# Attention probabilities of a two-layer hybrid block: the division by their sum, on the scalar engine instead of the vector engine

## The chip, the core and the metric

The kernel runs on one core of a Trainium2 chip. The metric is the device time of one execution in microseconds (us), of which the median of three runs is taken; it is 1531.88 us (1525.68 to 1533.71). One further execution was taken with the hardware profiler; all stretches and durations below are from that one. The engines of the core have short names: PE is the matrix engine (PEld its weight loads, which overlap with its multiplications), DVE the vector engine, ACT the scalar engine, POOL the GpSimd engine, SP the engine that issues most DMAs. Each engine works through its own instructions in the order in which they were written, and waits on semaphores for the others.

## The reference

Two layers over 256 latent tokens and 256 context tokens with 1024 channels, batch 1, float32. Each layer has three mixer branches (a bidirectional mLSTM, grouped-query attention and neighbourhood attention), their merge, and a convolutional feed-forward part. The change lies in the softmax that both attention branches use:

```python
def attend(q, k, v):
    s = jnp.einsum('bqkgd,bskd->bkgqs', q, k).astype(jnp.float32) * (HEAD_DIM ** -0.5)
    p = jax.nn.softmax(s, axis=-1).astype(v.dtype)
    return jnp.einsum('bkgqs,bskd->bqkgd', p, v)
...
def na_latent(q, k, v, kc, vc, rpb):
        ...
        s_win = jnp.einsum('bqhd,brqjhd->bhqrj', q_row, k_win).astype(jnp.float32) * scale + bias.astype(jnp.float32)
        s_ctx = jnp.einsum('bqhd,bshd->bhqs', q_row, kc).astype(jnp.float32) * scale
        s = jnp.concatenate([s_win.reshape(B, H, GRID_W, wr * wc), s_ctx], axis=-1)
        p = jax.nn.softmax(s, axis=-1).astype(v.dtype)
```

In both layers the latent tokens attend to latent and context tokens (512 keys); in layer 0 alone the context tokens also attend to themselves (256 keys).

## The kernel before, in words

**Large matrix products.** Every weight is loaded in float32 as a tile `raw` (two 128-row blocks of 512 columns, or one of 1024) and split into two float32r parts: `whi`, a cast by ACT (L200, `split_hi`), and `wlo`, the rest `raw - whi` by DVE (L204, `split_lo`). Each product is then three matmuls (L315, `mm3`): high by high, and the two mixed ones. One weight tile with its matmuls is a **piece**; `run` (L165) goes through all pieces in program order, and keeps the splits up to two pieces ahead of the matmuls that use them. After the matmuls of a piece, `run` advances a queue of side work by one step (`step`, L265). So side work stands between the pieces, on every engine, in the order in which Python wrote it: nothing is reordered later.

**Attention as side work.** `g_attend` (L651) is such a side task. Its **units** are a pair of heads by a block of 128 queries (512 keys), or in layer 0 also a pair of heads by all 256 context queries (`qt is None`, handled as two halves of 128x256 per head). Neighbourhood attention (`g_na`) and grouped-query attention (`g_gqa`) have 8 units of the first kind in each layer, and 4 of the second kind in layer 0. One step of the task t does three things, in this order:

- `pv` for unit t-2: the products of transposed probabilities `pT` with the values (L722), then the high part of the result on ACT (`yhi` or `y`, L725), and the low part on DVE (L726).
- `norm_transp` for unit t-1: four transposes on PE for each head of the pair (L708), from the probabilities `pr` into a PSUM bank, which is copied out as `pT` by ACT for the first head (L711) and by DVE for the second (L713).
- `scores` for unit t: the score products (L672, or L669 for the context units) into one bank for each head; then for each head on DVE the bias (L677, neighbourhood attention of the latent units only) and the negative maximum `mn` (L681), and on ACT the exponential with its row sum (L684); and after both heads, for each head, the reciprocal `rc` of the sum on DVE (L689) and the product `pr * rc` (L691).

Five banks are written in a step and four exist for side work (`bank(False)`). The second score product of a step therefore takes a bank that was used earlier in the same step: mostly the one of the first head's transposes, which is free once ACT has copied `pT` (L711), in some units the one of `pv`, which is free after L726.

**A piece and its step, in the order of the queues.** After a step of the attention, `run` splits the weights of a later piece: next on ACT stands `whi` (L200), next on DVE `wlo` (L204). In layer 0, pieces that only compute modulation vectors (L448, three DVE products of a 128x1024 weight tile with a vector) are spread among the others; they stand on DVE between the softmax of a step and the next `wlo`. When a block of pieces ends, ACT (or DVE) empties its banks; for the block of keys, values and gates of `g_gqa` these are four copies `akv` (L1156) on ACT, between `whi` and the next `yhi`.

**Draining.** A block that needs the output of a side task calls `finish`, which runs the rest of its steps with no pieces between them. In layer 0 the last context units of `g_gqa` are run so (the projection of that branch needs them).

In layer 0 a piece has matmuls for 512 token columns, in layer 1 the parts that only latent tokens need have 256, so pieces there are about half as long on PE, while a step of the attention is as long as in layer 0.

Of the kernel before, what the change touches and what calls it, by code (L numbers as in the profile page):

```python
# [13 lines left out]
ALU = mybir.AluOpType  # L14
# [34 lines left out]
class Builder:  # L49
# [601 lines left out]
    def g_attend(self, units, qk, v_of, y):  # L651


        nc = self.nc

        def scores(u):
            p, qt, c0, bias = u
            out = []
            bt = None
            if bias is not None:  # L660
                bt = self.t((128, 2, 256), name="nab")
                nc.gpsimd.dma_start(out=bt, in_=bias)
            bs = []
            for par in range(2):
                b = self.bank(False)
                q, k = qk(p, par)
                if qt is None:
                    for i in range(2):
                        nc.tensor.matmul(b[:, 256 * i:256 * i + 256], q[:, c0 + 128 * i:c0 + 128 * i + 128],  # L669
                                         k[:, 0:256], start=True, stop=True)  # L670
                else:
                    nc.tensor.matmul(b, q[:, c0:c0 + 128], k[:, 0:512], start=True, stop=True)  # L672
                bs.append(b)
            for par in range(2):
                b = bs[par]
                if bt is not None:
                    nc.vector.tensor_tensor(b[:, 256:512], b[:, 256:512], bt[:, par, :], op=ALU.subtract)  # L677
                mn = self.sm([128, 4], name="mn")
                ns = 2 if qt is None else 1
                w = 512 // ns  # L680
                nc.vector.tensor_reduce(mn[:, 0:ns], b.rearrange("p (n w) -> p n w", n=ns), axis=AX.X, op=ALU.min)  # L681
                pt = self.t(name="pr")
                for i in range(ns):
                    nc.scalar.activation(out=pt[:, w * i:w * i + w], in_=b[:, w * i:w * i + w], func=ACTF.Exp, scale=-1.0,  # L684
                                         bias=mn[:, i:i + 1], accum_out=mn[:, 2 + i:3 + i])
                rc = self.sm([128, 2], name="rc")
                out.append((pt, mn, rc, ns, w))
            for pt, mn, rc, ns, w in out:
                nc.vector.reciprocal(rc[:, 0:ns], mn[:, 2:2 + ns])  # L689
                for i in range(ns):  # L690
                    nc.vector.tensor_scalar(pt[:, w * i:w * i + w], pt[:, w * i:w * i + w], rc[:, i:i + 1], None,  # L691
                                            op0=ALU.mult)
            return [o[0] for o in out]

        def norm_transp(u, i):
            pts = res.pop(i)
            pT[i] = [transp(u, pts[par], par) for par in range(2)]

        def transp(u, pt, par):
            qt = u[1]  # L700
            b = self.bank(False)
            for i in range(4):
                if qt is None:

                    o = (i % 2) * 256 + (i // 2) * 128
                else:
                    o = i * 128
                nc.tensor.transpose(b[:, o:o + 128], pt[:, 128 * i:128 * i + 128], self.I)  # L708
            pT = self.t(name="pT")
            if par == 0:  # L710
                nc.scalar.copy(pT, b)  # L711
            else:
                nc.vector.tensor_copy(pT, b)  # L713
            return pT

        def pv(u, pTs):
            p, qt, c0, _ = u
            nkt, w = (2, 256) if qt is None else (4, 128)
            b = self.bank(False)
            for kt in range(nkt):  # L720
                for par in range(2):
                    nc.tensor.matmul(b[64 * par:64 * par + 64, 0:w], v_of(p, par, kt), pTs[par][:, w * kt:w * kt + w],  # L722
                                     start=kt == 0, stop=kt == nkt - 1)
            hi, lo = y[0][:, p, c0:c0 + w], y[1][:, p, c0:c0 + w]
            nc.scalar.copy(hi, b[:, 0:w])  # L725
            nc.vector.tensor_tensor(lo, b[:, 0:w], hi.bitcast(F32), op=ALU.subtract)  # L726

        n = len(units)
        res, pT = {}, {}
        for t in range(n + 2):  # L730
            if t >= 2:
                pv(units[t - 2], pT.pop(t - 2))
            if 1 <= t <= n:
                norm_transp(units[t - 1], t - 1)
            if t < n:
                res[t] = scores(units[t])
            yield
# [847 lines left out]
```

## Time and profile before

| | us |
|---|---|
| median of three runs | 1531.88 (1525.68 to 1533.71) |
| profiled execution, its own time | 1527.63 |
| span of its instructions | 1525.9 |
| DVE busy | 1090.3 (71%) |
| ACT busy | 732.1 (48%) |
| stretches with steps of neighbourhood attention | about 99 to 205 (layer 0), 1038 to 1093 (layer 1) |
| stretches with steps of grouped-query attention | about 265 to 363 (layer 0), 1122 to 1178 (layer 1) |

How the views are read: a *group* is all instructions of one source line, engine and shape, with its busy time, the mean duration of one in ns, and the idle time of the engine in front of it with what ended it. The *chain* is followed back from the last instruction of the span to what released each step. The *timeline* has start and duration of single instructions; neighbouring equal ones are merged (x4), and an idle time stands in brackets. Line numbers are those of the kernel before.

### The profile page before, as it was taken

How to read it: one execution, taken by the hardware profiler on the slowest of the kernel's cores; microseconds unless marked ns; L12 is line 12 of the kernel's file. 1: busy time of each engine (PE TensorE's matmuls, PEld its weight loads, DVE VectorE, ACT ScalarE, POOL GpSimd, SP SyncE). 2: the span in 40 equal slices, each digit the busy share in tenths (PEclk: the TensorE clock that was granted, in tenths of full speed). 3: DMA queues.
4: the chain of work that ended last, by engine and by line, in shares of the span. 5: the costliest groups of instructions: out<-in, count | busy, mean ns of one | idle time of the engine just before them, and what ended most of it. 6: DMA issues, size and time to landing. Idle time of an engine off the chain costs nothing.

```text
span 1525.9 us, 22991 instructions
## 1 busy us (share of the span) xinstructions
PE 1450.4 (95%) x8689; PEld 1251.4 (82%) x8689; DVE 1090.3 (71%) x1974; ACT 732.1 (48%) x1343; POOL 215.8 (14%) x312
## 2 busy tenths in 40 slices
PE   6999998998999899999999999999999998899997
PEld 3877787776888778888888887887887898899986
DVE  3548787777755887888767888736886347778874
ACT  4334441443435247644334555634554355666663
POOL 2000012003412031111011000000020230212110
PEclk9999999998999899999999999999999999999999
DMA  9624344331543356545554687733442344455662
GB/s 336 218 84 144 111 133 131 96 111 56 153 152 117 111 176 213 164 140 164 165 166 164 211 275 256 254 119 97 114 148 79 91 122 137 161 182 182 216 201 90
DMA packets 103807, 238.08 MB, mean 156 GB/s; under 512 B 8416, under 2 KB 18720, under 8 KB 103568
## 3 DMA queue, kind: packets, MB, share of 16 engines
q1 hardware_dynamic: 99472, 224.56, 45.7%
q0 software_dynamic: 4224, 12.05, 3.0%
q8 instruction: 68, 1.11, 0.3%
q14 instruction: 43, 0.35, 0.1%
HBM read 235.50 MB, written 1.08 MB: 155 GB/s over the span
## 4 chain that ended last, share of the span: by engine, by line
PE 71%; DVE 16%; ACT 5%; issue 4%; DMA 3%; POOL 1%; DVEq 0%; SPq 0%; ACTq 0%; POOLq 0%
PE bank L315 59%; DVE wlo L204 4%; PE bank L708 2%; PE bank L672 2%; PE bank L722 2%; DMA raw<-in_w_down 2%; DVE ta L1337 1%; DVE jnk L448 1%; ACT whi L200 1%; DVE D L1020 1%; ACT D L1003 1%; DVE raw L448 1%; PE bank L417 1%; PE bank L669 1%; DMA raw<-in_w_mod 1%
## 5 line engine op out<-in xcount | busy, mean ns | idle before, releaser
L204 DVE TENSOR_TENSOR wlo<-raw,whi 128x1024 fp32r<-128x1024 f32 (+1 forms) x330 | 410.9, 1260 | 154.0 <-ACT whi L200 152.9
L315 PE MATMUL bank<-HThi,whi 128*128 128x256 f32 (+1 forms) x1408 | 466.0, 331 | 7.8 <-DVE sig L1182 2.9
L315 PE MATMUL bank<-HThi,wlo 128*128 128x256 f32 (+1 forms) x1408 | 461.2, 328 | 7.7 <-DVE wlo L204 7.7
L315 PE MATMUL bank<-HTlo,whi 128*128 128x256 f32 (+1 forms) x1408 | 460.9, 327 | 0.5 <-DVE HTlo L591 0.5
L200 ACT CAST whi<-raw 128x1024 fp32r<-128x1024 f32 (+1 forms) x330 | 335.8, 1037 | 200.8 <-PE bank L315 60.7
L315 PEld LDWEIGHTS bank<-HThi,whi 128*128 128x128 f32 x1408 | 270.8, 192 | 39.2 <-issue 13.4
L315 PEld LDWEIGHTS bank<-HThi,wlo 128*128 128x128 f32 x1408 | 270.9, 192 | 27.6 <-DVE wlo L204 9.2
L315 PEld LDWEIGHTS bank<-HTlo,whi 128*128 128x128 f32 x1408 | 270.9, 192 | 18.9 <-DVE HTlo L591 1.2
L315 PE MATMUL bank<-whi,xs 128*128 128x512 f32 x528 | 160.1, 381 | 2.5 <-DVE o L623 1.6
L1337 DVE SCALAR_TENSOR_TENSOR ta<-bank,cw,ta 128x255 f32<-128x255 f32 (+2 forms) x224 | 110.7, 527 | 52.6 <-ACT ta L1334 48.6
L315 PE MATMUL bank<-whi,HThi 128*128 128x512 f32 (+1 forms) x384 | 143.3, 373 | 0.3 <-DVE sig L1182 0.2
L315 PE MATMUL bank<-wlo,HThi 128*128 128x512 f32 (+1 forms) x384 | 139.6, 364 | 0.8 <-DVE wlo L204 0.8
L315 PE MATMUL bank<-whi,HTlo 128*128 128x512 f32 (+1 forms) x384 | 139.4, 363 | 0.0
L315 PEld LDWEIGHTS bank<-whi,xs 128*128 128x128 f32 x528 | 99.8, 189 | 18.4 <-DVE o L623 2.0
L315 PE MATMUL bank<-wlo,xs 128*128 128x512 f32 x264 | 100.8, 382 | 4.3 <-DVE wlo L204 4.2
L448 DVE SCALAR_TENSOR_TENSOR raw<-raw,CB 128x1024 f32<-128x1024 f32 x80 | 102.2, 1277 | 1.7
L1357 POOL TENSOR_TENSOR hT<-ta 128x256 f32<-128x256 f32 (+1 forms) x48 | 60.2, 1257 | 303.5 <-ACT ta L1356 303.1
L684 ACT ACTIVATE pr<-bank,mn 128x512 f32<-128x512 f32 (+1 forms) x96 | 58.4, 614 | 91.4 <-DVE mn L681 85.0
L1334 ACT ACTIVATE ta<-bank,cw 128x256 f32<-128x256 f32 (+1 forms) x96 | 61.2, 646 | 84.3 <-PE bank L315 82.5
L315 PEld LDWEIGHTS bank<-whi,HThi 128*128 128x128 f32 x384 | 72.8, 190 | 21.6 <-issue 11.4
L315 PEld LDWEIGHTS bank<-wlo,HThi 128*128 128x128 f32 x384 | 72.9, 190 | 9.5 <-DVE wlo L204 1.5
L315 PEld LDWEIGHTS bank<-whi,HTlo 128*128 128x128 f32 x384 | 72.8, 189 | 8.7
(233 smaller groups left out, 1807.6 us busy)
## 6 DMA issues: line engine op xcount, KB each, us to landing
raw<-in_w_in SPq DMA_DIRECT2D x112, 512.0 KB, 3.7
raw<-in_w_up SPq DMA_DIRECT2D x96, 512.0 KB, 4.6
raw<-in_w_modT SPq DMA_DIRECT2D x80, 512.0 KB, 4.5
raw<-in_w_down SPq DMA_DIRECT2D x66, 512.0 KB, 4.6
raw<-in_w_branch SPq DMA_DIRECT2D x24, 512.0 KB, 3.7
raw<-in_w_out SPq DMA_DIRECT2D x24, 512.0 KB, 4.3
raw<-in_w_mod SPq DMA_DIRECT2D x16, 512.0 KB, 10.5
nab<-in_nabias POOLq DMA_DIRECT2D x16, 256.0 KB, 3.2
```

What stands on the lines that cost most here:

```text
L200: nc.scalar.copy(p.hi, p.raw.tile[:, p.k0:p.k0 + p.kn, :])
L204: nc.vector.tensor_tensor(p.lo, p.raw.tile[:, p.k0:p.k0 + p.kn, :], p.hi.bitcast(F32), op=ALU.subtract)
L315: nc.tensor.matmul(out, l, self.woven(r), start=first and i == 0, stop=last and i == 2)
L417: nc.tensor.matmul(st["b"][32 * g:32 * g + 32, 256 * ch:256 * ch + 256], w, rt[:, g, :], start=c == 0, stop=c == 1)
L448: nc.vector.scalar_tensor_tensor(o, rt[:, 0, a:b], 1.0, self.CB[:, s, a:b], op0=ALU.mult, op1=ALU.mult, accum_out=acc)
L672: nc.tensor.matmul(b, q[:, c0:c0 + 128], k[:, 0:512], start=True, stop=True)
L684: nc.scalar.activation(out=pt[:, w * i:w * i + w], in_=b[:, w * i:w * i + w], func=ACTF.Exp, scale=-1.0, bias=mn[:, i:i + 1], accum_out=mn ...
L708: nc.tensor.transpose(b[:, o:o + 128], pt[:, 128 * i:128 * i + 128], self.I)
L722: nc.tensor.matmul(b[64 * par:64 * par + 64, 0:w], v_of(p, par, kt), pTs[par][:, w * kt:w * kt + w], start=kt == 0, stop=kt == nkt - 1)
L1334: nc.scalar.activation(out=tv, in_=bv, func=ACTF.Identity, scale=cw[:, ch, 1:2], bias=cw[:, ch, 3:4])
L1337: nc.vector.scalar_tensor_tensor(o, x, cw[:, ch, t:t + 1], o, op0=ALU.mult, op1=ALU.add)
L1357: nc.gpsimd.tensor_tensor(hv, av, ta, op=ALU.mult)
```

## The change

The product L691 moves from DVE to ACT. Its inputs, its output and its place in the program text stay, so on ACT it stands behind the exponentials of both heads of the unit, and ahead of everything that is written later. The product has a scale that is a column of numbers in memory (one for each partition), not a constant.

```diff
             for pt, mn, rc, ns, w in out:
                 nc.vector.reciprocal(rc[:, 0:ns], mn[:, 2:2 + ns])
                 for i in range(ns):
-                    nc.vector.tensor_scalar(pt[:, w * i:w * i + w], pt[:, w * i:w * i + w], rc[:, i:i + 1], None,
-                                            op0=ALU.mult)
+                    nc.scalar.mul(pt[:, w * i:w * i + w], pt[:, w * i:w * i + w], rc[:, i:i + 1])
             return [o[0] for o in out]
```

Later lines of the changed kernel have numbers that are lower by one.

ACT, neighbourhood attention in layer 1, around the copies `akv`, before:

```order
L684 ACTIVATE pr,mn<-bank,mn 128x512 x2
L200 CAST whi<-raw 128x1024
L1156 COPY akv<-bank 128x272 x4
L725 CAST y<-bank 128x128
L711 COPY pT<-bank 128x512
L684 ACTIVATE pr,mn<-bank,mn 128x512 x2
L200 CAST whi<-raw 128x1024
```

The same place on ACT, after:

```order
L684 ACTIVATE pr,mn<-bank,mn 128x512 x2
L691 ACTIVATE pr<-pr,rc 128x512 x2
L200 CAST whi<-raw 128x1024
L1155 COPY akv<-bank 128x272 x4
L724 CAST y<-bank 128x128
L710 COPY pT<-bank 128x512
L684 ACTIVATE pr,mn<-bank,mn 128x512 x2
L691 ACTIVATE pr<-pr,rc 128x512 x2
L200 CAST whi<-raw 128x1024
```

Two products stand between the exponentials of a unit and the next cast `whi`; the casts, the copies `akv`, and the `y` and `pT` of the next step stand behind them. No load of a function table is added on ACT.

DVE, one turn of the neighbourhood attention in layer 1, before:

```order
L677 TENSOR_TENSOR bank<-bank,nab 128x256
L681 TENSOR_REDUCE mn<-bank 128x1
L677 TENSOR_TENSOR bank<-bank,nab 128x256
L681 TENSOR_REDUCE mn<-bank 128x1
L689 RECIPROCAL rc<-mn 128x1
L691 TENSOR_SCALAR pr<-pr,rc 128x512
L689 RECIPROCAL rc<-mn 128x1
L691 TENSOR_SCALAR pr<-pr,rc 128x512
L204 TENSOR_TENSOR wlo<-raw,whi 128x1024
L726 TENSOR_TENSOR y<-bank,y 128x128
L713 COPY pT<-bank 128x512
```

The same turn on DVE, after:

```order
L677 TENSOR_TENSOR bank<-bank,nab 128x256
L681 TENSOR_REDUCE mn<-bank 128x1
L677 TENSOR_TENSOR bank<-bank,nab 128x256
L681 TENSOR_REDUCE mn<-bank 128x1
L689 RECIPROCAL rc<-mn 128x1 x2
L204 TENSOR_TENSOR wlo<-raw,whi 128x1024
L725 TENSOR_TENSOR y<-bank,y 128x128
L712 COPY pT<-bank 128x512
```

The products are gone from between the reciprocals, and `wlo`, which needs `whi`, still stands ahead of the low part `y`, the copy `pT` and the bias of the next unit. The orders of PE, POOL and SP do not change.

## The prediction

> **What bounds the kernel now.** I read the page first: the busy times, then the chain that ended last.
>
> ```profile
> PE 1450.4 (95%) x8689; PEld 1251.4 (82%) x8689; DVE 1090.3 (71%) x1974; ACT 732.1 (48%) x1343; POOL 215.8 (14%) x312
> PE 71%; DVE 16%; ACT 5%; issue 4%; DMA 3%; POOL 1%; DVEq 0%; SPq 0%; ACTq 0%; POOLq 0%
> ```
>
> PE holds the end nearly everywhere; DVE holds 16% of the chain, ACT 5%. So the question is not what DVE and ACT do in sum, but in which stretch of the attention one of them keeps PE waiting. Second, the groups of the product and of the ACT operations nearest to its new form:
>
> ```profile
> L691 DVE TENSOR_SCALAR pr<-pr,rc 128x512 f32<-128x512 f32 x64 | 31.2, 487 | 2.2
> L691 DVE TENSOR_SCALAR pr<-pr,rc 128x256 f32<-128x256 f32 x32 | 9.9, 351 | 0.6
> L1356 ACT ACTIVATE ta<-ta 128x512 f32<-128x512 f32 x18 | 11.4, 631 | 13.7 <-DVE ta L1337 13.7
> L1356 ACT ACTIVATE ta<-ta 128x256 f32<-128x256 f32 x30 | 12.3, 417 | 15.8 <-DVE ta L1337 15.4
> L1037 ACT ACTIVATE H<-bank,mr 128x128 f32<-128x128 f32 x24 | 8.7, 363 | 48.9 <-DVE mr L1035 47.5 <-PE bank L1031 0.7
> L725 ACT CAST y<-bank 128x128 fp32r<-128x128 f32 x16 | 4.3, 270 | 16.8 <-PE bank L722 16.7
> L1334 ACT ACTIVATE ta<-bank,cw 128x512 f32<-128x512 f32 x36 | 28.1, 781 | 47.1 <-PE bank L315 47.1
> L1174 ACT ACTIVATE sig<-bank 128x512 f32<-128x512 f32 x24 | 13.6, 603 | 10.2 <-PE bank L315 10.2
> ```
>
> DVE spends 31.2 + 9.9 = 41.1 us on the product. Third, the waits of PE: the product ends 9.1 us of PE's idle time.
>
> ```profile
> PE bank L708 <- DVE pr L691: 9.1, 11, 1.6
> ```
>
> Fourth, the chain and the timelines of the attention stages, quoted where they are used.
>
> **The change: the price of one product on ACT.** The trace has no product of this form on ACT. An in-place function on 128x512 took 0.631 us with constant scale (L1356). A column as scale costs 0.363 - 0.270 = 0.09 (L1037 against L725, same size, both from PSUM). I take 0.631 + 0.09 = 0.72, and 0.417 + 0.09 = 0.51 for 128x256; the lower bound is 0.63, the upper is 0.78 (L1334, two columns). ACT starts the next operation about 0.1 before the end of the last: three L1174 took 1.59,
>
> ```profile
> 194.75 1.59 ACT L1174 ACTIVATE sig<-bank 128x512 f32<-128x512 f32 x3
> ```
>
> that is (1.59 - 0.60)/2 = 0.50 each beside a duration of 0.60. A product thus holds ACT for 0.62 (0.53 to 0.68), a small one for 0.41, and `whi` moves back by 2 x 0.62 = 1.24 us in a unit of 512 keys. ACT has room for it in sum: 64 x 0.62 + 32 x 0.41 = 53 us on an engine that is 48% busy. What counts is the order.
>
> **Layer 1, neighbourhood attention: the main term.** Chain, one turn on PE, and the same turn on DVE and ACT:
>
> ```profile
> 1070.32 1.42 PE bank L672 x4
> ...
> 1076.57 1.42 PE bank L672 x4
> ```
>
> ```profile
> 1071.41 0.43 DVE L677 TENSOR_TENSOR bank<-bank,nab 128x256 f32<-128x256 f32 x1 [0.36 <-PE bank L672]
> ...
> 1075.56 1.23 DVE L204 TENSOR_TENSOR wlo<-raw,whi 128x1024 fp32r<-128x1024 f32 x1 [0.25 <-ACT whi L200]
> 1076.70 0.29 DVE L726 TENSOR_TENSOR y<-bank,y 128x128 fp32r<-128x128 f32 x1
> 1076.90 0.68 DVE L713 COPY pT<-bank 128x512 f32<-128x512 f32 x1
> 1077.66 0.43 DVE L677 TENSOR_TENSOR bank<-bank,nab 128x256 f32<-128x256 f32 x1
> ```
>
> ```profile
> 1073.81 0.69 ACT L684 ACTIVATE pr<-bank,mn 128x512 f32<-128x512 f32 x1 [0.34 <-DVE rc L689]
> 1074.39 0.19 ACT L684 ACTIVATION_READ_ACCUMULATOR pr<-bank,mn 128x1 f32 x1
> 1074.48 1.04 ACT L200 CAST whi<-raw 128x1024 fp32r<-128x1024 f32 x1
> ```
>
> PE's turn is 1076.57 - 1070.32 = 6.25. Beside it runs a ring through DVE and ACT: bias to second exponential 2.40, exponential to `whi` 0.67, `whi` to `wlo` 1.08, then `wlo` 1.14, `y` 0.20 and `pT` 0.60 (DVE, too, starts the next some 0.08 early), and the next bias may start: 6.09. Its slack against PE is only 0.16. The removed DVE products are not in this ring (DVE then waits 0.25 for `whi` anyway), so nothing is gained; the two ACT products are: 6.09 + 1.24 = 7.33, or **1.08 more than PE's turn**. From the third unit's bias to the eighth's there are five such turns:
>
> ```profile
> 1052.17 0.43 DVE L677 TENSOR_TENSOR bank<-bank,nab 128x256 f32<-128x256 f32 x1 [0.36 <-PE bank L672]
> ...
> 1083.91 0.43 DVE L677 TENSOR_TENSOR bank<-bank,nab 128x256 f32<-128x256 f32 x1 [0.18 <-PE bank L672]
> ```
>
> They now take 31.74, and will take 5 x 7.33 = 36.65: +4.9. The two units ahead, whose casts are half as wide, add about 0.85 by the same walk (the first waits for both exponentials ahead of its product, then a ring of 6.3 against 6.1). Of the 5.75 on DVE, PE absorbs about 0.25 at the last unit: **+5.5 us**, 4.1 to 6.3 with the bounds of the product. Behind it PE runs on without gaps until the next chain, so nothing gives it back.
>
> **Layer 1, grouped-query attention.** No bias, so the ring is shorter. Chain of a turn:
>
> ```profile
> 1133.52 1.06 PE bank L672 x4
> ...
> 1139.51 1.42 PE bank L672 x4
> ```
>
> ```profile
> 1129.43 0.69 ACT L684 ACTIVATE pr<-bank,mn 128x512 f32<-128x512 f32 x1 [0.91 <-DVE mn L681]
> 1130.11 0.68 ACT L684 ACTIVATE pr<-bank,mn 128x512 f32<-128x512 f32 x1
> 1130.77 1.04 ACT L200 CAST whi<-raw 128x1024 fp32r<-128x1024 f32 x1
> ```
>
> ```profile
> 1128.71 1.28 DVE L681 TENSOR_REDUCE mn<-bank 128x1 f32<-128x512 f32 x2
> ```
>
> PE's turn is 5.99. The ring, from `mn` to `mn`: 0.72 to the first exponential, 0.68 to the second, 0.66 to `whi`, and the same rest, 1.08 + 1.14 + 0.20 + 0.60: 5.08; with 1.24 it is 6.32. In the first turn the second score product waits for `pT` of ACT, which I estimate at 0.3 to spare and which comes 1.24 later (about +1.0); the three turns behind add 0.33 each, less the slack of their score products (+0.5): **+1.5** (0.7 to 2.2). The last turns are those of whole-width pieces, as in layer 0 below, and lose nothing.
>
> **Layer 0, neighbourhood attention.** At its start DVE is the bound, and here the product does go: the second one stood between `rc` and the modulation product.
>
> ```profile
> 112.57 0.16 DVE L689 RECIPROCAL rc<-mn 128x1 f32<-128x1 f32 x1 [0.31 <-ACT pr L684]
> 112.77 0.49 DVE L691 TENSOR_SCALAR pr<-pr,rc 128x512 f32<-128x512 f32 x1
> 113.17 0.69 DVE L448 SCALAR_TENSOR_TENSOR jnk<-raw,CB 128x512 f32<-128x512 f32 x1
> ```
>
> That is 0.4 for each of two units: -0.8 on DVE. The third has no modulation product, so its `wlo` waits for `whi`: +1.24 - 0.8 = +0.4. Then the unit with the copies `akv`, where ACT has no gap:
>
> ```profile
> 127.14 1.25 ACT L1156 COPY akv<-bank 128x272 f32<-128x272 f32 x4
> ...
> 128.40 0.64 ACT L711 COPY pT<-bank 128x512 f32<-128x512 f32 x1
> ```
>
> ```profile
> 129.09 0.29 PEld L672 LDWEIGHTS bank<-nk,nq 64*128 64x128 f32 x2 [0.78 <-ACT pT L711]
> ```
>
> The second score product already waits 0.78 for `pT`; `pT` moves by 0.4 + 1.24: **+1.65** (1.1 to 2.0). After that PE's turn is 8.84,
>
> ```profile
> 154.24 1.02 PE bank L708 x8
> ...
> 163.08 1.02 PE bank L708 x8
> ```
>
> and the ring, 7.33, stays below it: 0. At the end of the grouped-query attention three units run with nothing between them.
>
> ```profile
> 345.02 0.17 DVE L689 RECIPROCAL rc<-mn 128x2 f32<-128x2 f32 x1
> 345.23 0.62 DVE L691 TENSOR_SCALAR pr<-pr,rc 128x256 f32<-128x256 f32 x2
> ```
>
> DVE ends the four products 0.8 after the last exponential frees `rc`; on ACT they take 4 x 0.41 + 0.1 = 1.7. Against +0.9 in each of the last two stands the 0.5 that DVE gains in the first, and what overlaps with the transposes: **+0.8** (0 to 1.5).
>
> **Sum.** 5.5 + 1.5 + 1.65 + 0.8 = +9.5 us, bounds 5.9 and 12.0. The profiled execution's own time is 1527.63, so it would be 1537.1. The median of the runs shown is 4.25 above it; on that, 1531.9 + 9.5 = **1541.4**, which I forecast.
>
> **The rivals.**
>
> - *Not slower: the rings don't bind.* If the products cost ACT less, or the split ran further ahead, so that the added 1.24 fitted, only the gain at the start (-0.8) and a stall at the copies would be left: -1.2 to +1, about 1531.9. For it: ACT is idle half the time. It decides at 0.16 us: as long as two products lengthen the ring by less, PE keeps its 6.25. Against it: the lower bound is 2 x 0.53.
> - *Faster: DVE's relief reaches the end.* If every wait of PE for the product (9.1) went and its DVE stretches shrank by two units' products (2), it would be 1520.8. Against it: PE's wait is for the probabilities, which still have to be multiplied, and later than before.
> - *Every product shows at the end with its extra length*: 64 x (0.72 - 0.49) + 32 x (0.51 - 0.35) = 20 us, 1551.9. Against it: most units stand where PE's turn is over 8 us. The Trainium skill (ScalarE: Activation LUTs, section Rules for kernel authors) gives multiplications to VectorE as the faster engine; taken as a rule for this kernel it means this case, while the rows agree on the two prices but show most of them hidden.
>
> That the products do move, with no added table load, stands in the order of the built program.
>
> **How the numbers follow.** Forecast 0.68, rings don't bind 0.18, all shown 0.07, relief 0.07. A measurement tells 0.5% (7.7 us) from no change. Of the forecast's range 5.9 to 12.0 about four fifths lies above 7.7, so slower by over 0.5% is 0.68 x 0.8 + 0.07 = 0.61, within 0.5% 0.18 + 0.14 = 0.32, faster 0.07. The range takes in the forecast with its bounds, the spread of the runs before, and the unbound rings: 1530 to 1548; the relief and the case in which all shows are left out.
>
> **What would show it.** Right: in layer 1 the biases L677 stand 7.2 to 7.5 apart instead of 6.25, DVE's idle time ahead of `wlo` grows from 0.25 to over 1 with ACT `whi` as its end, PE waits for ACT `pr` ahead of the transposes, and the stretch from 1038 to 1093 is 4 to 6 us longer; the product takes 0.70 to 0.73. Wrong: biases 6.25 apart, or a product under 0.6; or a gain in layer 0 that outweighs layer 1, with DVE's chain from 104 to 121 shorter by more than 1 and no new wait at 129. The forecast falls if `wlo` does not wait for `whi` in that ring.

## The result, and the profile after

| | before | after |
|---|---|---|
| median of nine runs each, us | 1526.60 (1524.46 to 1533.71) | 1538.64 (1535.00 to 1545.81) |
| ratio, 95% interval | | 1.0076 (1.0058 to 1.0094) |
| span of the profiled execution, us | 1525.9 | 1535.9 |

The change costs 0.76%, by the ratio 11.6 us (8.9 to 14.4); the two profiled spans are 10.0 apart. First the engines' sums on the page of the changed kernel:

```profile
PE 1461.1 (95%) x8689; PEld 1253.5 (82%) x8689; DVE 1047.4 (68%) x1878; ACT 779.9 (51%) x1439; POOL 215.1 (14%) x312
```

DVE did become 43 us less busy, and ACT 48 us more (before: 1090.3 and 732.1). Neither gives the time. The groups of the product in its new place:

```profile
L691 ACT ACTIVATE pr<-pr,rc 128x512 f32<-128x512 f32 x64 | 42.4, 712 | 0.0
L691 ACT ACTIVATE pr<-pr,rc 128x256 f32<-128x256 f32 x32 | 13.6, 512 | 0.0
```

712 and 512 ns, where DVE had 487 and 351. Where the time went is seen in layer 1. One turn of the neighbourhood attention in the timeline of DVE after (start, duration, instruction, and in brackets the idle time in front of it with what ended it):

```profile
1078.77 0.42 DVE L677 TENSOR_TENSOR bank<-bank,nab 128x256 f32<-128x256 f32 x1
...
1081.91 0.17 DVE L689 RECIPROCAL rc<-mn 128x1 f32<-128x1 f32 x1 [0.86 <-ACT pr L684]
1084.07 1.23 DVE L204 TENSOR_TENSOR wlo<-raw,whi 128x1024 fp32r<-128x1024 f32 x1 [2.00 <-ACT whi L200]
1085.21 0.28 DVE L725 TENSOR_TENSOR y<-bank,y 128x128 fp32r<-128x128 f32 x1
1085.41 0.68 DVE L712 COPY pT<-bank 128x512 f32<-128x512 f32 x1
1086.01 0.42 DVE L677 TENSOR_TENSOR bank<-bank,nab 128x256 f32<-128x256 f32 x1
```

The same turn on ACT:

```profile
1081.10 0.69 ACT L684 ACTIVATE pr<-bank,mn 128x512 f32<-128x512 f32 x1 [0.29 <-DVE rc L689]
...
1081.78 1.32 ACT L691 ACTIVATE pr<-pr,rc 128x512 f32<-128x512 f32 x2
1083.00 1.03 ACT L200 CAST whi<-raw 128x1024 fp32r<-128x1024 f32 x1
```

The two products stand 1.22 us (1083.00 - 1081.78) ahead of `whi`. DVE, which has lost its own two products, now idles 2.00 ahead of `wlo` (0.25 before): what was taken from it turned into waiting. Because `wlo` comes late, so do `y`, `pT` and the bias of the next unit, which no longer waits for PE: it stands 7.24 behind the last one (1086.01 - 1078.77) instead of 6.25. PE's loss is seen at its weight loads in that turn:

```profile
1082.54 0.42 PEld L707 LDWEIGHTS bank<-ident,pr 128*128 128x128 f32 x4 [0.35 <-ACT pr L691]
...
1084.73 0.29 PEld L672 LDWEIGHTS bank<-nk,nq 64*128 64x128 f32 x2 [0.70 <-ACT pT L710]
```

They wait 0.35 for the product and 0.70 for `pT`, which ACT copies only after `whi`. In the kernel before, the transposes and score products of such a turn stood only behind 0.16 to 0.17 of issue:

```profile
1075.48 0.86 PEld L708 LDWEIGHTS bank<-ident,pr 128*128 128x128 f32 x8 [0.17 <-issue]
1076.50 0.66 PEld L672 LDWEIGHTS bank<-nk,nq 64*128 64x128 f32 x4 [0.16 <-issue]
```

PE itself counts these waits as busy, since the ends of its matmuls are modelled, so the page has it busier after (1461.1) than before (1450.4). Over the whole stage, the first and the eighth bias of the changed kernel:

```profile
1043.54 0.43 DVE L677 TENSOR_TENSOR bank<-bank,nab 128x256 f32<-128x256 f32 x1 [10.01 <-PE bank L672]
...
1093.21 0.42 DVE L677 TENSOR_TENSOR bank<-bank,nab 128x256 f32<-128x256 f32 x1
```

and the first of the kernel before (its eighth, at 1083.91, stands in the prediction):

```profile
1039.59 0.43 DVE L677 TENSOR_TENSOR bank<-bank,nab 128x256 f32<-128x256 f32 x1 [10.01 <-PE bank L672]
```

49.67 us instead of 44.32: **+5.35** in this stage alone. In the grouped-query attention of layer 1 the eight minima L681 span 49.86 instead of 46.36: **+3.50**. There the chain shows something that the prediction had not. A turn on DVE after:

```profile
1145.18 1.28 DVE L681 TENSOR_REDUCE mn<-bank 128x1 f32<-128x512 f32 x2
...
1149.58 1.23 DVE L204 TENSOR_TENSOR wlo<-raw,whi 128x1024 fp32r<-128x1024 f32 x1 [1.99 <-ACT whi L200]
1150.72 1.41 DVE L1181 SCALAR_TENSOR_TENSOR sig<-sig,bank 128x256 f32<-128x256 f32 x4
1152.05 0.28 DVE L725 TENSOR_TENSOR y<-bank,y 128x128 fp32r<-128x128 f32 x1
1152.25 0.68 DVE L712 COPY pT<-bank 128x512 f32<-128x512 f32 x1
1152.85 1.28 DVE L681 TENSOR_REDUCE mn<-bank 128x1 f32<-128x512 f32 x2
```

In two of the turns four instructions that empty PE's banks into `sig` stand between `wlo` and `y`, and add 1.33 (1152.05 - 1150.72) to the ring: 7.67 here, and 7.61 in the other, where the other turns of half-width pieces have 6.1 to 6.35. The kernel before has them at the same place:

```profile
1134.62 1.29 DVE L681 TENSOR_REDUCE mn<-bank 128x1 f32<-128x512 f32 x2 [0.36 <-PE bank L672]
...
1138.95 1.40 DVE L1182 SCALAR_TENSOR_TENSOR sig<-sig,bank 128x256 f32<-128x256 f32 x4
...
1141.08 1.28 DVE L681 TENSOR_REDUCE mn<-bank 128x1 f32<-128x512 f32 x2
```

This turn took 6.46 (1141.08 - 1134.62), and the minimum at its end has no idle time in front of it: with 5.08 + 1.33 = 6.41 the ring was the bound here already, so the whole delay of `whi` came on top.

In layer 0 the loss is at the copies `akv`. The timeline of PE's weight loads after, and the stretches behind it (length; busy time and count of PE, PEld, DVE, ACT, POOL; granted PE clock; DMA share and GB/s):

```profile
130.92 0.29 PEld L672 LDWEIGHTS bank<-nk,nq 64*128 64x128 f32 x2 [1.86 <-ACT pT L710]
```

```profile
130.00:132.00 2.00, 1.08 (x2) 0.29 (x2) 1.98 (x4) 0.87 (x3) 0.00 (x0) 0.95 0.77 232
132.00:134.00 2.00, 2.00 (x6) 1.57 (x6) 1.79 (x4) 0.89 (x3) 0.00 (x0) 0.50 0.97 380
134.00:136.00 2.00, 2.00 (x8) 1.65 (x7) 1.27 (x4) 2.00 (x5) 0.00 (x0) 0.69 0.12 47
```

The wait for `pT` grew from 0.78 to 1.86, the way forecast though by 1.08 and not by 1.65; but behind it PE ran at half its clock, 0.50, until about 135, and had 6 matmuls in 2 us where the kernel before has 11. That cost another 1.7 us (2 x (0.05 + 0.50 + 0.31)). It is taken up below.

### The profile page after: what moved, and what is told of

It reads as the page before. It is cut to its first block, busy times and chain, and to the rows that moved or that the text cites. A ratio compares the mean times of both kernels' runs of the same rounds, so it can differ in the third digit from the quotient of the medians.

```text
span 1535.9 us, 22927 instructions
## 1 busy us (share of the span) xinstructions
PE 1461.1 (95%) x8689; PEld 1253.5 (82%) x8689; DVE 1047.4 (68%) x1878; ACT 779.9 (51%) x1439; POOL 215.1 (14%) x312
## 3 DMA queue, kind: packets, MB, share of 16 engines
HBM read 235.50 MB, written 1.08 MB: 154 GB/s over the span
## 4 chain that ended last, share of the span: by engine, by line
PE 64%; DVE 17%; ACT 8%; issue 5%; DMA 4%; POOL 1%; DVEq 0%; SPq 0%; ACTq 0%; POOLq 0%
PE bank L315 55%; DVE wlo L204 4%; DMA raw<-in_w_down 3%; ACT whi L200 2%; PE bank L721 2%; PE bank L707 2%; PE bank L672 1%; ACT pr L684 1%; DVE ta L1336 1%; DVE jnk L448 1%; DVE mn L681 1%; ACT pr L691 1%; DVE D L1019 1%; ACT D L1002 1%; DVE raw L448 1%
```

## The experiments

The totals are ratios to the kernel before, with 95% intervals, in us of its time. Each interval is about 2 to 3 us to either side, so single turns say more than totals; the experiments were made so that turns differ.

### The parts one by one

One condition chooses the engine of L691; everywhere else the product is on DVE. For e1_na1 (in e2_gqa1 `br != NA`, in e3_l0 `l == 0`):

```diff
+                    if l == 1 and br == NA:
+                        nc.scalar.mul(pt[:, w * i:w * i + w], pt[:, w * i:w * i + w], rc[:, i:i + 1])
+                    else:
+                        nc.vector.tensor_scalar(pt[:, w * i:w * i + w], pt[:, w * i:w * i + w], rc[:, i:i + 1], None,
+                                                op0=ALU.mult)
```

> The product is on ACT only in the neighbourhood attention of layer 1; everywhere else it stays on DVE. Theory (the cast `whi` is late): the two products hold ACT for 2 x 0.61 = 1.22 us ahead of `whi`, and the ring bias, exponential, `whi`, `wlo`, `y`, `pT` is the bound there: biases L677 7.2 us apart, DVE idle about 2.0 ahead of `wlo`, the stretch from the first scores to the end of the last +5.2, and nothing is lost or gained elsewhere: total +5.2 (4.3 to 6.0). Rival (price): each product costs what it is longer by, 0.712 - 0.487 = 0.225: turns of 6.25 + 0.45 = 6.70, total 16 x 0.225 = +3.6. Rival (given back): the loss is regained behind 1093 because the next stage has slack: the stretch +5.2, the total under +2.

> The product is on ACT only in the grouped-query attention of layer 1. Theory (the cast is late, and in two turns the 1.40 us of L1182, `sig` on DVE, come into the ring because it stands between `wlo` and `y`): turns of 6.3 and, with `sig`, of about 7.65 instead of 5.99; the stretch +3.5, total +3.5 (2.5 to 4.2). Rival (the first walk, without `sig`): all turns 6.3, +1.5. Rival (price): 16 x 0.225 = +3.6 with no turn over 6.5; the lengths of the turns tell it from the theory.

> The product is on ACT in layer 0 only (both branches). Up to the end of layer 0 the program is that of the changed kernel. Theory: +1.65 at the copies `akv`, +1.0 at the three drained units, nothing in between: +2.7; layer 1 as before. On PE's half clock behind the gap at 130 (1.5 us in the changed kernel's profile) two views differ: if the gap itself brings it, it is here again at the same place, and the total is +4.2 (3.5 to 5.0); if it falls at random on gaps of PE, it may be missing here, with the total at +2.7 (1.5 to 3.5), and it comes at other gaps. Rival (price): 48 x 0.225 + 32 x 0.16 = +11 (the units of 128 queries and the context units).

| | ratio | us | its stage in the profile |
|---|---|---|---|
| e1_na1 | 1.0036 (1.0014 to 1.0057) | +5.5 | turns 7.2 to 7.5, but the first, second and fifth 7.69, 7.03 and 8.27; +7.83 |
| e2_gqa1 | 1.0009 (0.9994 to 1.0025) | +1.4 | turns 6.1 to 6.4, with `sig` 7.67 and 7.61; +3.50 |
| e3_l0 | 1.0018 (1.0003 to 1.0032) | +2.7 | neighbourhood attention +2.46, half clock at 130 to 134 again |

The sum of the three, +9.6, is within the error of the whole change, +11.6. The turns are the theory's, not those of the price (6.70) nor of the walk without `sig` (all 6.3); and +2.7 (0.5 to 4.9) in layer 0 is far below the price's +11, though it can't tell the two views on the half clock apart. The total of e2_gqa1 alone can't be told from nothing.

In e1_na1 the stage has 2.48 more than in the changed kernel, nearly all of it in those three turns, though the program is the same there:

```profile
1045.00:1050.00 5.00, 3.30 (x18) 1.52 (x16) 1.65 (x4) 3.84 (x9) 0.54 (x1) 0.88 0.07 8
1050.00:1055.00 5.00, 5.00 (x42) 4.65 (x40) 2.38 (x6) 3.15 (x7) 0.00 (x0) 0.78 0.40 149
...
1070.00:1075.00 5.00, 4.14 (x10) 2.20 (x9) 4.18 (x8) 3.13 (x10) 0.15 (x1) 0.77 0.56 157
1075.00:1080.00 5.00, 5.00 (x35) 3.83 (x34) 2.38 (x4) 3.15 (x7) 0.66 (x2) 0.89 0.09 11
```

These are two stretches of half clock, each worth 5 x (0.12 + 0.22) = 1.7 us. The profiled execution of e1_na1 has 32 us of such loss over its span, that of the kernel before 23, of the changed kernel 24.5 (the missing share of the clock, summed over the span). It was also the longest of its twelve runs (1540.99, median 1534.25).

The mean granted clock is on record for every run of the experiments, and with it the loss (1 - clock) x span. Over the 86 runs of the kernel before, made beside the experiments, it lies between 18 and 29 us, and the span grows by 1.03 us for each us of it: what one execution differs in from the next is mostly half clock. So the means of a kernel can be parted in two. Against the runs of the kernel before beside them:

| | longer, us | of it half clock | the rest |
|---|---|---|---|
| e1_na1 | 5.0 | 0.7 | 4.3 |
| e2_gqa1 | 1.5 | -2.4 | 3.9 |
| e3_l0 | 2.9 | 2.3 | 0.6 |

These are good to about 1 or 2 us. The rest of e2_gqa1 fits the +3.50 of its stage and the forecast, which its total does not show.

### The delay of `whi`, or the product?

e4_dummy keeps the products on DVE and gives ACT idle ones of the same size:

```diff
                     nc.vector.tensor_scalar(pt[:, w * i:w * i + w], pt[:, w * i:w * i + w], rc[:, i:i + 1], None,
                                             op0=ALU.mult)
+                    nc.scalar.mul(self.scr[:, w * i:w * i + w], self.CB[:, 0, w * i:w * i + w], rc[:, i:i + 1])
```

> The kernel before, products on DVE, with as many idle products added on ACT: the same sizes and the same column as scale, from a constant tile into a scratch tile in bf16 that nobody reads, at the place where the change puts the product. It leaves out nothing; DVE does all it did. Theory (what counts is that the cast `whi` stands behind them): layer 1 as slow as with the change, biases 7.2 apart, +5.2 in the neighbourhood attention and +3 in the grouped-query attention; in layer 0 the start loses what DVE's relief gave as well (+0.8 more): total +10 to +13. Rival (the product itself comes late for the transposes): the transposes have their probabilities as early as before, so 0 to +2. Rival (relief counts): much slower than with the change, over +15.

1.0099 (1.0078 to 1.0120), +15.1 us (11.9 to 18.3); the span is 14.6 longer, of which about 5 are more half clock. On DVE, the turn in layer 1:

```profile
1081.45 0.49 DVE L692 TENSOR_SCALAR pr<-pr,rc 128x512 f32<-128x512 f32 x1
1082.27 0.17 DVE L690 RECIPROCAL rc<-mn 128x1 f32<-128x1 f32 x1 [0.34 <-ACT pr L685]
1082.47 0.48 DVE L692 TENSOR_SCALAR pr<-pr,rc 128x512 f32<-128x512 f32 x1
1084.57 1.23 DVE L205 TENSOR_TENSOR wlo<-raw,whi 128x1024 fp32r<-128x1024 f32 x1 [1.61 <-ACT whi L201]
```

The probabilities are ready at 1082.95 and DVE still idles 1.61 for `whi`. The turns are 7.35 to 7.6, 0.14 above those of the change, since the second idle product waits for a reciprocal that stands behind DVE's first product. So the loss in layer 1 needs no product on ACT, only work of that length ahead of `whi`. The total is above the theory's 13, which its interval takes in, and touches the second rival's 15; over its runs 2.8 of the 14.9 us that the mean is longer are half clock, and the rest, 12.1, is the theory's. That the reciprocal is what adds the 0.14 is read from the order and was not tested.

e8_one puts only the first head's product on ACT:

```diff
+                    if pt is out[0][0]:
```

> Only the first head's product of each pair is on ACT, the second head's stays on DVE. Theory (delay of `whi`): `whi` 0.61 later, ring 6.09 + 0.61 = 6.7: biases in layer 1 6.6 to 6.8 apart, neighbourhood attention +2.0 (1.5 to 2.8), grouped-query attention +1.2 (two turns with `sig` at 7.0, the others 6.0), copies `akv` +1.0, drained units 0 to +0.5 (both engines share the four products): total +4 to +5. Rival (proportional): half of everything the change cost, +5.8 by the ratio, with turns 6.75. Rival (ACT and DVE side by side do the pair sooner): no loss, -1 to +1.

1.0017 (1.0002 to 1.0031), +2.6 us. The biases:

```profile
1081.07 0.42 DVE L677 TENSOR_TENSOR bank<-bank,nab 128x256 f32<-128x256 f32 x1
...
1087.66 0.42 DVE L677 TENSOR_TENSOR bank<-bank,nab 128x256 f32<-128x256 f32 x1
```

6.59 here, 6.59 to 6.86 in the five turns of this kind; with `sig` 7.06 and 7.01: the forecast of `whi` 0.61 later. The total is below the forecast's +4, which its interval takes in. The drained units lost more than forecast: PE waits 2.12, 0.99 and 2.10 for ACT's product there.

e5_drop has neither product:

```diff
-                for i in range(ns):
-                    nc.vector.tensor_scalar(pt[:, w * i:w * i + w], pt[:, w * i:w * i + w], rc[:, i:i + 1], None,
-                                            op0=ALU.mult)
```

> The product is left out on both engines, so the probabilities stay unnormalised; the reciprocal stays. What it isolates is the relief of DVE alone, with nothing added on ACT. Theory (DVE's product was hidden nearly everywhere): turns of the neighbourhood attention in layer 1 as before (6.25 to 6.45), turns of the grouped-query attention as before, about 1 us gained at the start of layer 0 and under 1 at the drained units: total -1 to -3. Rival (relief): the 9.1 us that PE waits for the product and the two shortened DVE stretches are regained: -8 to -11.

0.9937 (0.9919 to 0.9955), -9.6 us: my theory missed here, and the rival's number came out. The turns in layer 1 are the old ones but for the first (6.1 to 6.5; the first 5.79, 0.71 shorter), as the theory says; but in three places PE waits for the product itself: in the first three units of layer 0 (3.9 us in all), in the first unit of layer 1 (1.14), and in the drained units (4.1). In the timeline of PE before, the drained units:

```profile
344.81 0.63 PE L708 MATMUL bank<-ident,pr 128*128 128x128 f32 x4 [1.55 <-DVE pr L691]
...
359.29 0.63 PE L708 MATMUL bank<-ident,pr 128*128 128x128 f32 x4 [1.55 <-DVE pr L691]
```

Here nothing lies between exponential, product and transpose. Without the product PE waits 2.4 in all for exponentials, where it had waited 9.1 for products:

```profile
PE bank L705 <- ACT pr L684: 2.4, 7, 0.4
```

Three stretches of half clock between 344 and 360 go too. Over its runs 5.5 of the 9.8 us that the mean is shorter are less half clock; only the rest, 4.3, can be the waits themselves. This is what leaving the product out is worth, not what moving it can bring: after the change PE's waits for it are 9.0, and those of the transposes' weight loads, 3.2 before, are 17.2.

### The order on ACT

e6_hi_first writes the next `whi` ahead of a unit's exponentials. `run` gets a function that casts the next weight tile if the next round would do so anyway; `g_attend` calls it behind the copies `pT`:

```diff
+        def early_hi():
+            k, n = state["split"], self.cur + 1
...
+            q = prog[k]
+            held = ahead - (1 if prog[n].split and k > n else 0)
+            if q.split and not q.hold and q.pre is None and q.hi is None and q.lo is None and held < 2 and not prog[k - 1].fence:
+                split_hi(q)
...
+            self.early_hi()
             if t < n:
                 res[t] = scores(units[t])
```

> The changed kernel (products on ACT), with the next cast `whi` written ahead of the unit's exponentials and products, behind the copy `pT`, where the next piece allows it: in layer 1 in every unit, in layer 0 in about every second one, and not in the unit with the copies `akv`. Theory (only the place of `whi` behind the products cost time): the turns in layer 1 fall back to PE's 6.25 to 6.5 and 5.9 to 6.5; the neighbourhood attention there +0 instead of +5, the grouped-query attention +0 instead of +3.5; the copies `akv` and the drained units keep their +1.65 and +1.0: total +1 to +3 against the kernel before. Rival (the product comes late for the transposes, or ACT is full in the ring whatever the order): the turns stay at 6.9 or more, total +7 to +10.

0.9988 (0.9977 to 1.0000), -1.8 us. The turn in layer 1, on DVE:

```profile
1074.55 0.43 DVE L690 TENSOR_TENSOR bank<-bank,nab 128x256 f32<-128x256 f32 x1 [0.36 <-PE bank L685]
...
1077.83 1.21 DVE L204 TENSOR_TENSOR wlo<-raw,whi 128x1024 fp32r<-128x1024 f32 x1
1079.13 0.29 DVE L738 TENSOR_TENSOR y<-bank,y 128x128 fp32r<-128x128 f32 x1
1079.69 0.69 DVE L725 COPY pT<-bank 128x512 f32<-128x512 f32 x1 [0.27 <-PE bank L720]
1080.74 0.43 DVE L690 TENSOR_TENSOR bank<-bank,nab 128x256 f32<-128x256 f32 x1 [0.36 <-PE bank L685]
```

`wlo` waits for nothing, and the bias waits for PE again: 6.19. The same products on the same engine cost next to nothing in layer 1 once `whi` is ahead of them: +0.35 and +0.32 in the two stages, instead of +5.35 and +3.50. Only the first turn of the neighbourhood attention is as long as with the change (7.00). The total is lower than the forecast +1 to +3. In layer 0 the wait at `akv` (1.85) and the half clock behind it are still there.

e7_hi_first_dve has that order with the products on DVE.

> The kernel before (products on DVE), with `whi` written ahead of the exponentials as in e6_hi_first. Theory: in layer 1 PE's turn binds before already (slack 0.16 in the ring), so the neighbourhood attention gains 0 to 0.5, the two turns of 6.4 with `sig` in the grouped-query attention may fall to 6.0 (-0.8), layer 0 about 0: total -2 to 0. Rival (`whi` held PE back in many more places than the chain shows): -4 or more.

0.9989 (0.9976 to 1.0001), -1.7 us, within the forecast; by the total it can't be told from e6_hi_first. In layer 1 its stages are 0.56 and 0.31 shorter than there: that is what the products on ACT cost, in one profile each, once `whi` is out of their way.

e11_hi_mid calls the same function between exponentials and products:

```diff
+            self.early_hi()
             for pt, mn, rc, ns, w in out:
                 nc.vector.reciprocal(rc[:, 0:ns], mn[:, 2:2 + ns])
```

> The changed kernel, with `whi` between the exponentials and the products of a unit instead of behind both, so `whi` is as early as in the kernel before and the products are 0.95 us later than with the change. Theory (two rings): the ring over `whi` is back at 6.1, but the one over the product binds: bias to second exponential 2.40, exponential 0.67, `whi` 0.95, products 1.32, transposes 1.02, first score product to bias 1.1: 7.46; biases in layer 1 7.3 to 7.6 apart, total as with the change or above it, +9 to +14. Rival (only the place of `whi` counts, the products have room behind it): turns 6.25 to 6.5 as in e6_hi_first, total -2 to +3.

1.0081 (1.0061 to 1.0101), +12.4 us. ACT, and then PE's weight loads, in layer 1:

```profile
1083.73 1.03 ACT L200 CAST whi<-raw 128x1024 fp32r<-128x1024 f32 x1
1084.66 1.33 ACT L705 ACTIVATE pr<-pr,rc 128x512 f32<-128x512 f32 x2
```

```profile
1085.44 0.42 PEld L721 LDWEIGHTS bank<-ident,pr 128*128 128x128 f32 x4 [1.24 <-ACT pr L705]
1086.05 0.42 PEld L721 LDWEIGHTS bank<-ident,pr 128*128 128x128 f32 x4 [0.20 <-ACT pr L705]
```

`wlo` now waits 0.77 instead of 2.00, but PE waits 1.24 for the product, which is ready 1.4 later than in the kernel before, and the turns of this kind are 7.04 to 7.48. So there are two rings in the neighbourhood attention, one over `whi` and `wlo`, one over the product and the transposes, and neither has room for 1.2 us more. Of the three places that were tried, only the one ahead of both, while ACT waits for `mn`, is free. In the grouped-query attention the second ring has more room: behind the first, the turns are 6.15 to 6.5 here, those with `sig` too (6.46 and 6.40).

### The unit at the copies, and the half clock

e9_akv is the changed kernel with the products of the unit ahead of `akv` on DVE:

```diff
+                    if not (l == 0 and br == NA and t == 3):
```

> The changed kernel, with the products of one unit alone, the one ahead of the copies `akv` in layer 0 (the fourth of the neighbourhood attention), back on DVE. Theory: `pT` of that unit comes 1.2 to 1.65 us earlier, PE's idle time ahead of the second score product shrinks from 1.86 to about 0.8 (PEld), and PE's half clock behind it (132 to 135, 1.5 us) goes too: end of the neighbourhood attention of layer 0 at +0 instead of +2.9 against the kernel before; total about 2.5 to 3.2 below the changed kernel (+7 to +9 against the kernel before). Rival (the half clock has nothing to do with that gap): only the 1.65 goes, the end of that stretch stays at +1.3 or more.

The stage is as forecast: PEld waits 0.77 for `pT`, no half clock follows, and the neighbourhood attention of layer 0 ends 0.45 earlier than in the kernel before, not 2.9 later. The total missed: 1.0078 (1.0060 to 1.0096), +11.9, where +7 to +9 was forecast. Its profile has 29 us of half-clock loss against the changed kernel's 24.5, at other places; over its runs 3.9 us of the difference are half clock, and the rest is 7.5. What of this belongs to the program, the last experiment asks.

e12_again is the changed kernel itself, once more.

> The changed kernel itself a second time, on the chip of the day: what of its profile repeats and what does not. Theory (turns are set by the order of the queues, the half clock by chance on gaps of PE): the same turns in layer 1 to 0.1 us (7.2 to 7.5 and 6.3/7.65), PEld's wait for `pT` at the copies `akv` 1.85 again; the stretches of half clock, each worth 1.7 us, in part at other places than in the first profile, their sum between 22 and 32 us; ratio 1.006 to 1.010. Rival (the half clock belongs to the program's gaps alone): the same stretches at the same places as in the first profile (24, 128, 248, 348, 520, 908, 992, 1340).

1.0090 (1.0067 to 1.0113), +13.7 us. First and eighth bias:

```profile
1038.86 0.43 DVE L677 TENSOR_TENSOR bank<-bank,nab 128x256 f32<-128x256 f32 x1 [10.01 <-PE bank L672]
...
1088.52 0.42 DVE L677 TENSOR_TENSOR bank<-bank,nab 128x256 f32<-128x256 f32 x1
```

49.66 us (49.67 in the first profile), and the grouped-query turns agree to 0.02. At `akv` the wait is the same, but what follows is not:

```profile
130.09 0.29 PEld L672 LDWEIGHTS bank<-nk,nq 64*128 64x128 f32 x2 [1.85 <-ACT pT L710]
```

```profile
132.00:134.00 2.00, 2.00 (x11) 1.76 (x10) 1.11 (x5) 1.69 (x5) 0.00 (x0) 1.00 0.63 232
```

The clock is 1.00 and PE does 11 matmuls in 2 us. The stretches at 24, 128, 248, 908 and 992 of the first profile are missing here, and there are others at 1208 and 1292, so the rival is out: the turns belong to the program, the places of the half clock in part to the execution. How much there is of it does depend on the program: over these six runs 28.0 us, beside them in the kernel before 22.6.

### The two places put right

e10_best is e6_hi_first with the products of that unit and of the drained units on DVE:

```diff
+                    if not (l == 0 and (t == 3 if br == NA else t >= 9)):
```

> The kernel of e6_hi_first (products on ACT, `whi` ahead of the exponentials), with the products of the unit ahead of the copies `akv` and of the last three context units, which run with nothing between them, back on DVE. Theory (the losses of e6_hi_first were these two places): end of the neighbourhood attention of layer 0 -0.5 to -1.2 against the kernel before, drained units +0, layer 1 as in e6_hi_first: total -2 to -5. Rival (e6_hi_first has nothing left to gain): as e6_hi_first, -0.5 to -2.

0.9976 (0.9962 to 0.9990), -3.7 us, median 1523.12: below both kernels. At the end of layer 0's neighbourhood attention it is 2.8 ahead of the kernel before, of which it had 0.9 before the attention began. Over its runs 2.6 of the 3.9 us that the mean is shorter are less half clock. That it is better than e6_hi_first or e7_hi_first_dve is not shown: the intervals overlap.

## Why the prediction was right, and where it was not

| term | forecast | profile after | second profile |
|---|---|---|---|
| neighbourhood attention, layer 1 | +5.5 | +5.35 | +5.34 |
| grouped-query attention, layer 1 | +1.5 | +3.50 | +3.49 |
| layer 0, start and copies `akv` | +1.65 | +2.46 | +0.81 |
| drained units | +0.8 | about +1.0 | about +1.1 |
| elsewhere | 0 | -2.3 | -1.7 |
| span | +9.5 | +10.0 | +9.0 |

- **Price of the product: right.** 0.72 and 0.51 were forecast from two neighbouring groups and the column as scale; 0.712 and 0.512 came, and `whi` moved by 1.22 instead of 1.24.
- **The ring in layer 1: right.** The five turns of whole casts are 7.20 to 7.47 against 7.33, together 36.34 against 36.65, the two ahead of them add 0.75 against 0.85, and `whi` ends DVE's wait. e4_dummy and e6_hi_first show it as the cause from both sides: delay without the move costs at least as much, the move without the delay costs next to nothing there.
- **Grouped-query attention: mis-sized.** The failed step is "the three turns behind add 0.33 each": the ring was walked without the 1.33 of `sig`, which I had not seen in two of the turns. They grew by 1.21 and 1.19, since the ring with `sig` bound them already; the others by 0.38 and 0.50, so there were four turns behind the first and not three; the first grew by 1.23 (+1.0 forecast). In the whole-width turns, which the sum put at nothing, 1.31 came back in the first and 0.30 was added in the last. In place of +1.5 the stage shows +3.50.
- **Layer 0: the mechanism right, the size open by 1.7.** The row counts from 95 to 205, less what stood at 95. In both profiles PE loses 1.2 to 1.3 us in the unit at the copies (the wait for `pT` grows by 1.07 and 1.08) and 0.15 in the units ahead of it (forecast 1.24 and 0.4). About 0.5 comes back at 173, in a context unit, where PE's weight loads for the score products take 1.28 before and 0.74 after. That fits a relief of DVE, which the sum put at nothing there: the same 0.5 comes back in e3_l0, e5_drop and e9_akv, in which DVE has lost these products too, and not in e1_na1, e2_gqa1 and e7_hi_first_dve, in which it keeps them. So the second profile, in which PE keeps its clock, ends at +0.81; in the first, half clock (1.7) stands on top.
- **Drained units: right**, within what half clock there lets one read.
- **"So nothing gives it back"** is right behind the neighbourhood attention of layer 1, where the difference falls by no more than 0.35 until the next attention. The -2.3 elsewhere is a sum of larger parts, which can be followed along PE's weight loads, as they come in the same order in both kernels. Half clock at other places cancels in it: one stretch fewer at 520 and one behind 1190, one more at 908 and at 992. But between 912 and 950 the difference falls from 4.8 to 1.8 us; there ACT's casts wait for the DMA of the weights, 22.7 us before and 14.1 after (900 to 960). In the second profile that stretch gives back 0.8.
- **The total: in part luck.** The span came out at +10.0 against +9.5 because the +2.0 that the grouped-query attention was mis-sized by and the half clock at `akv` stand against that -2.3. The median of 1538.64 lies 2.8 below the forecast 1541.4, but the forecast started from the median of three runs, 1531.88, where nine have 1526.60; the change itself is 11.6 by the ratio, 2 more than forecast.
- **The rivals.** Rings that don't bind: the turns exclude it. Every product with its extra length: 20 us against 11.6 (8.9 to 14.4) measured; the Trainium skill's rule (ScalarE: Activation LUTs, Rules for kernel authors) that multiplications belong on VectorE points the right way, but its reason, the price, is not the cause: with `whi` moved, e6_hi_first pays the price and loses next to nothing. The relief: moving brings next to none, since the waits for the product are 9.1 before and 9.0 after; e5_drop shows that those waits were worth something.

That the ratios came out at 11.6 and 13.7 us while the terms sum to 9.5 is, by the clocks on record, more half clock on average. The two profiles, with 24.5 and 23 us of it against 23 before, show little of that: the fifteen runs of the changed kernel lose 26.7 us to it on average (error 1.0), the 86 of the kernel before 23.8 (0.2). In e12_again the mean is 12.7 us longer, of which 5.3 are half clock and 7.3 the rest; the prediction had no term for it. That the change brings it by giving PE more gaps is likely, since the kernels with late products or casts (e4_dummy, e9_akv, e11_hi_mid) have 2.8 to 4.7 us more than the kernel before and e5_drop, with fewer waits, 5.5 less; no run shows it gap by gap.

## What to carry to other kernels

Moving an operation to an idle engine delays everything written behind it on that engine; look for what there is waited for by the engine that was relieved, and follow that ring to its start. Here DVE got rid of 0.97 us of products per unit and idled 1.75 longer, until the cast behind them was moved ahead, into ACT's wait for `mn`. And compare the turns of single stages before totals: the turns repeated to 0.02 us, while a total is known to 2 or 3. Where totals must do, take the loss by the granted clock of each run out of them first.

## What the runs showed of the hardware

PE's granted clock falls to 0.50 for stretches of 3.4 us, which cost 1.7 us each where PE is the bound. Those followed here begin 0.6 to 1.7 us behind a short wait. At the copies `akv`, where PEld waited 1.73 to 1.86, four of six profiles show a stretch right behind (the changed kernel's first, e3_l0, e6_hi_first, e11_hi_mid) and two do not (the second, e4_dummy); where it waited 0.67 to 1.38, none of eight does. Behind a gap of 1.22 at 1200, the kernel before had one, and the changed kernel did not behind the same gap at 1212.

The Trainium skill (TensorE: Matmul & The Clock Gate, HAM oscillation) gives gaps over about 3.4 us as the rule of thumb for this; here half clock followed a gap of 1.03 in PE's matmuls (1.86 in its weight loads), so the measurement goes further than the rule. What it says of a window that runs freely (Part 1: The HAM clock gate) fits that the same gap meets it in one execution and not in the next; no run here shows the window itself.
